# An mLSTM chunk updates its state right behind the numerators, and turns its normalised rows behind the next dense tile

## The chip, the cores and the metric

The kernel runs on one core of a Trainium2 chip. TensorE (PE) multiplies matrices; VectorE (DVE), ScalarE (ACT) and GpSimd (POOL) work on tiles; SyncE (SP) issues most of the transfers between HBM and the on-chip memory SBUF. PSUM holds the products of TensorE until another engine has read them. The metric is the time of one execution on the device in microseconds, as the median of several runs.

## The reference

The reference is one inference step of a decoder of two layers, for 1,024 prompt tokens and 8 samples of one token each. Layer 0 projects the normalised input once, runs a Mamba-2 scan (16 heads) and an mLSTM scan (4 heads of 256) side by side, and projects both together; layer 1 is an RWKV-7 time mixing; a SwiGLU stands behind each. The change concerns the mLSTM scan over chunks of 128 tokens, of which this is the core (c and n are the carried state):

```python
s = einsum('bthd,bshd->btsh', qc, kc) * exp(dlog - m_t[:, :, None])
num = einsum('btsh,bshv->bthv', s, vc) + w_inter[..., None] * einsum('bthd,bhdv->bthv', qc, c)
den = sum(s, axis=2) + w_inter * einsum('bthd,bhd->bth', qc, n)
h = num / maximum(abs(den), exp(-m_t))[..., None]
...
c = dc[..., None, None] * c + einsum('bshd,bshv->bhdv', ws[..., None] * kc, vc)
n = dc[..., None] * n + einsum('bsh,bshd->bhd', ws, kc)
```

Each head's 256 values of h are then normalised by their root mean square, gated and projected.

## The kernel before

Everything runs on one core, layer after layer. The large products are dense tiles of 128 output rows (`dense_tile`), each in three passes of a high and a low part (`mm3`): 24 matmuls for one block of columns, three blocks of 344 columns (72 matmuls) in the z and o tiles of the input projection, one block of 512 in the out tiles of the output projection. Dense tiles use a ring of three PSUM buffers (psd), everything else in layer 0 a ring of five (psb, through `bank`).

The eight mLSTM chunks are strewn among the dense tiles, in this order: chunk 0, three z tiles, chunk 1, three z tiles, a part of the Mamba output, chunk 2, four o tiles, chunk 3, four o tiles, chunk 4, eight out tiles, chunk 5, `mix_ml` (which reads the rows of chunks 0 to 3), eight out tiles, chunk 6, and, from within the first SwiGLU, chunk 7 and the samples.

A chunk (`ml_chunk`) does the following. It loads its queries, keys and values and two broadcast rows of gate logarithms, BM and WI. DVE computes `ws` from the last column of BM, ACT its exponential; POOL and ACT turn BM into the decay matrix. TensorE computes the scores (`sc`, L689), turns the keys into rows (`kT`), and computes the four numerators (`num`, L709 and, from chunk 1 on, L712 with the state `Cst`); each lies in a bank of its own, with the denominator as its last column. For each head ACT takes the absolute value of the denominator into `dn`, DVE copies the numerator into `hr` (L714), and ACT sums its squares into `ss` (with `junk` as the discarded output). `ml_norm_tok` then computes one factor per row and head from `dn` and `ss`: five short operations of DVE (L145, L658) and a logarithm and an exponential on ACT. DVE multiplies `hr` by it, head by head (L151). TensorE turns the rows in eight transposes into two banks (`hT`, L724), ACT copies them to SBUF (L725), and a transfer stores them to HBM. Last, eight products `cu` (L731), two for each head, carry the state forward: each is evacuated by DVE, in chunk 0 as a copy into `Cst` (L734), later by one operation that scales the old state and adds the product (L148).

The buffers: qc, BM and WI have two each, so the load for chunk c+2 begins when chunk c has read its own for the last time; hr, hT, kc, va, vw and the transposed keys have one each. The order of instructions on each engine isn't the order of the program text: a scheduler replays the program against a model of the engines and lists each engine's instructions by when they could start there, with the text's order as priority. Every engine then starts its instructions in the listed order, and each waits for what it needs. Names in the trace carry no chunk numbers: `hr`, `cu` and so on stand for all chunks. L145, L148 and L151 are helpers (`tt`, `stt`, `ts`) that issue one operation each, and L154 is `act`; L186 is the matmul in `mm3`.

Of the kernel before, what the change touches and what calls it, by code (L numbers as in the profile page):

```python
# [8 lines left out]
F32 = mybir.dt.float32  # L9
# [15 lines left out]
LCH = 128  # L25
# [65 lines left out]
def _body(tc, nc, I, O, top):  # L91
# [20 lines left out]
    V, S, G, PE, SY = nc.vector, nc.scalar, nc.gpsimd, nc.tensor, nc.sync  # L112
    dma = SY.dma_start
# [20 lines left out]
    ident = cst("ident")  # L134
# [3 lines left out]
    def bank(name):  # L138
        return P_.b.tile([128, 512], F32, name=name, tag="bank")
# [7 lines left out]
    def stt(out, a, s, b, op0=ALU.mult, op1=ALU.mult, e=None):  # L147
        (e or V).scalar_tensor_tensor(out=out, in0=a, scalar=s, in1=b, op0=op0, op1=op1)  # L148

    def ts(out, a, s1, op0=ALU.mult, s2=None, op1=ALU.bypass, e=None):  # L150
        (e or V).tensor_scalar(out=out, in0=a, scalar1=s1, scalar2=s2, op0=op0, op1=op1)  # L151
# [14 lines left out]
    def wload(src, name, n=1024, step=128, e=None, th=TA_, p=128):  # L166
# [11 lines left out]
                out.append((hi[0:p, q:q + step], lo[0:p, q:q + step]))  # L178
        return out

    def mm3(ps, terms):
        n = 3 * len(terms)
        i = 0
        for w, x in terms:
            for a, b in ((0, 1), (1, 0), (0, 0)):
                PE.matmul(out=ps, lhsT=w[a], rhs=x[b], start=i == 0, stop=i == n - 1)  # L186
                i += 1

    def dense_tile(w, xs, name, evac, m=128, blocks=NBLK, base=0, th=TA_):

        for n0, n in blocks:
            ps = th.bank(f"ps_{name}_{n0}")
            o = ps[0:m, 0:n]
            c = slice(n0 - base, n0 - base + n)
            mm3(o, [(wk, (x[0][:, c], x[1][:, c])) for wk, x in zip(w, xs)])
            evac(n0, n, o)

    def dbank(name):
        return psd.tile([128, 512], F32, name=name, tag="d")
# [455 lines left out]
    def ml_norm_tok(dn, ss, enm, rows, name):  # L655

        tt(dn, dn, enm, ALU.max)
        V.reciprocal(out=dn, in_=dn)  # L658
        tt(ss, ss, dn)
        tt(ss, ss, dn)  # L660
        act(ss, ss, AF.Ln, scale=1.0 / 256, bias=eps[0:rows, :])
        act(ss, ss, AF.Exp, scale=-0.5)
        tt(ss, ss, dn)

    def ml_chunk(c):
# [40 lines left out]
        for h in range(4):  # L706
# [6 lines left out]
            act(dn[:, h:h + 1], b[:, 256:257], AF.Abs)  # L713
            V.tensor_copy(out=hr[:, h, :], in_=b[:, 0:256])  # L714
            act(junk, hr[:, h, :], AF.Square, accum_out=ss[:, h:h + 1])
        ml_norm_tok(dn, ss, tokb[:, c, 32:36], 128, f"{c}")
        for h in range(4):
            ts(hr[:, h, :], hr[:, h, :], ss[:, h:h + 1])
        hT = mp_.tile([128, 8, 128], F32, name=f"hT{c}", tag="hT", bufs=1)
        for hf in range(2):  # L720
            b = bank("hT")
            for q in range(4):
                i = hf * 4 + q
                PE.transpose(b[:, q * 128:q * 128 + 128], hr[:, i // 2, (i % 2) * 128:(i % 2) * 128 + 128], ident)  # L724
            S.copy(hT[:, hf * 4:hf * 4 + 4].rearrange("p c d -> p (c d)"), b)  # L725
        dma(out=HMT[:, :, t0:t0 + LCH], in_=hT)
        for h in range(4):
            for k in range(2):
                b = bank("cu")
                o = b[:, 0:257]  # L730
                PE.matmul(out=o, lhsT=ktok[:, (2 * h + k) * 128:(2 * h + k) * 128 + 128], rhs=vw[:, h, :],  # L731
                          start=True, stop=True)
                if c == 0:
                    V.tensor_copy(out=Cst[:, h, k, :], in_=o)  # L734
                else:
                    stt(Cst[:, h, k, :], Cst[:, h, k, :], WI[:, h, 127:128], o, ALU.mult, ALU.add)


    def ml_decode(dp):
# [21 lines left out]
        qms = [mp_.tile([128, 8, 32], F32, name=f"qm{i}", tag=f"qm{i}", bufs=1) for i in range(2)]  # L761
        for qm in qms:
            G.memset(qm, 0.0)
        hsr = mp_.tile([128, 256], F32, name="hsr", tag="hr", bufs=1)
        nc_acc = mp_.tile([128, 257], F32, name="nc_acc", tag="nc_acc", bufs=1)
        yield
        for b_ in range(8):
# [1046 lines left out]
```

## Time and profile before

| | us |
|---|---|
| median of 3 runs | 3504.39 (3503.94 to 3506.5) |
| profiled execution, its own time | 3510.93 |
| span of the profiled execution | 3509.2 |
| TensorE busy in the span | 3245.9 |
| VectorE busy | 2333.7 |
| ScalarE busy | 1653.4 |
| GpSimd busy | 1241.3 |
| from 490 to 870 us, where the mLSTM chunks lie: TensorE waiting for `hr` | 13.2 |

The profile is one execution of the program, and this one took 6.5 us more than the median. Its mean granted TensorE clock was 0.967 of full speed. Rows of a timeline give an instruction's start, its duration and its engine, line, operation and operands; xN at the end is a run of N of them, and the bracket gives the idle time before and what ended it. Rows of windows give, for each stretch, its length and each engine's busy time in it, and at the end the granted clock, the busy share of the DMA engines and their GB/s. Rows of waits give who waited for what, for how long in total, how often, and the longest.

### The profile page before, as it was taken

What the parts mean: (1) busy time and instruction counts of PE and PEld (TensorE: products, weight loads), DVE (VectorE), ACT (ScalarE), POOL (GpSimd) and SP (SyncE); (2) the same over time, 40 slices, a digit from 0 to 9 for tenths busy, and PEclk for the clock granted to TensorE, in tenths of its full rate; (3) what the DMA queues carried; (4) which work ended last, traced back from release to release, by engine and by line L of the source; (5) the groups of instructions that cost most, each with busy time, mean ns of one, the idle gap of its engine ahead of it and who ended that gap; (6) DMA issues with size and microseconds to landing.
All of it is one profiled execution on the core that took longest, in us unless ns stands there. A gap on an engine that the chain in (4) does not pass through costs nothing.

```text
span 3509.2 us, 61245 instructions
## 1 busy us (share of the span) xinstructions
PE 3245.9 (92%) x22615; PEld 3000.7 (86%) x22615; DVE 2333.7 (67%) x4315; ACT 1653.4 (47%) x3701; POOL 1241.3 (35%) x1586
## 2 busy tenths in 40 slices
PE   6998899998999999989999968988989999999998
PEld 6987789877778887779999968987888889999998
DVE  8865744466765477676776686667777776575555
ACT  5444435434243245654454555665555644453223
POOL 3257520121200002254644566237677783000000
PEclk9999999999999999999999989998999999999999
DMA  3467665663663343553333324462433333333232
GB/s 117 123 183 217 212 194 150 185 196 128 224 198 109 96 144 108 183 153 98 102 102 94 99 77 131 133 204 73 116 100 98 100 95 109 125 97 97 85 102 67
DMA packets 399135, 458.26 MB, mean 131 GB/s; under 512 B 154756, under 2 KB 295524, under 8 KB 398708
## 3 DMA queue, kind: packets, MB, share of 16 engines
q1 hardware_dynamic: 398836, 454.34, 43.6%
q8 instruction: 179, 2.93, 0.3%
q14 instruction: 120, 0.98, 0.1%
HBM read 352.10 MB, written 102.07 MB: 129 GB/s over the span
## 4 chain that ended last, share of the span: by engine, by line
PE 48%; DVE 11%; POOL 10%; DMA 7%; ACT 5%; issue 4%; SPq 1%; DVEq 0%; ACTq 0%; POOLq 0%
PE ps_g L186 10%; PE ps_u L186 9%; PE ps_d L186 8%; PE ps_rw L186 6%; POOL X L145 4%; POOL t L145 4%; PE ps_out L186 3%; PE ps_o L186 2%; ACT L154 2%; PE ps_wo L186 1%; PE M L1361 1%; DMA phm<-scr_hmt 1%; PE cu L731 1%; PE sc L1361 1%; DMA obd<-scr_tblk 1%
## 5 line engine op out<-in xcount | busy, mean ns | idle before, releaser
L186 PE MATMUL ps_d<-al,dhi 128*128 128x260 f32 (+2 forms) x1248 | 386.5, 310 | 20.4 <-DVE xa L145 6.3
L186 PE MATMUL ps_d<-ah,dhi 128*128 128x260 f32 (+2 forms) x1248 | 373.9, 300 | 0.0
L186 PE MATMUL ps_d<-ah,dlo 128*128 128x260 f32 (+2 forms) x1248 | 373.6, 299 | 0.0
L145 POOL TENSOR_TENSOR X<-X,t 32x30 f32<-32x30 f32 (+14 forms) x480 | 308.6, 643 | 32.7
L145 POOL TENSOR_TENSOR t<-X 32x30 f32<-32x30 f32 (+14 forms) x480 | 297.6, 620 | 30.5
L186 PEld LDWEIGHTS ps_d<-al,dhi 128*128 128x128 f32 x1248 | 237.9, 191 | 40.5 <-DVE xa L145 10.7
L186 PEld LDWEIGHTS ps_d<-ah,dlo 128*128 128x128 f32 x1248 | 238.3, 191 | 7.3
L186 PEld LDWEIGHTS ps_d<-ah,dhi 128*128 128x128 f32 x1248 | 237.9, 191 | 7.3 <-issue 0.2
L145 DVE TENSOR_TENSOR wlo_g<-raw_g,whi_g 128x512 fp32r<-128x512 f32 (+1 forms) x192 | 143.2, 749 | 112.9 <-ACT whi_g L175 105.7
L948 ACT CAST dhi<-rawd 128x1024 fp32r<-128x1024 f32 x88 | 88.4, 1046 | 211.5 <-PE ps_d L186 204.9
L175 ACT CAST whi_g<-raw_g 128x512 fp32r<-128x512 f32 (+1 forms) x192 | 114.0, 599 | 147.7 <-DMA raw_g<-in_wgu 90.6
L154 ACT ACT_TABLE_LOAD x136 | 174.5, 1283 | 6.4 <-DVE ss L145 4.1
L145 DVE TENSOR_TENSOR wlo_u<-raw_u,whi_u 128x512 fp32r<-128x512 f32 x176 | 134.6, 766 | 58.1 <-ACT whi_u L175 57.2
L175 ACT CAST whi_u<-raw_u 128x512 fp32r<-128x512 f32 x176 | 108.0, 619 | 122.7 <-PE ps_u L186 97.4
L186 PE MATMUL ps_in<-xnl,whi_in 128*128 128x344 f32 x480 | 156.4, 326 | 1.0 <-ACT ext L287 1.0
L186 PE MATMUL ps_in<-xnh,whi_in 128*128 128x344 f32 x480 | 155.7, 324 | 0.0
L186 PE MATMUL ps_in<-xnh,wlo_in 128*128 128x344 f32 x480 | 155.3, 324 | 0.0
L145 DVE TENSOR_TENSOR dlo<-rawd,dhi 128x512 fp32r<-128x512 f32 x176 | 128.2, 782 | 15.6 <-ACT dhi L948 15.6
L145 POOL TENSOR_TENSOR xx<-xa 128x512 f32<-128x512 f32 x8 | 9.7, 1244 | 350.7 <-PE ps_out L186 350.7
L157 ACT CAST ah<-sg 128x260 fp32r<-128x260 f32 (+2 forms) x155 | 67.5, 436 | 139.4 <-DVE sg L148 137.6
L145 POOL TENSOR_TENSOR Bb<-Bc,consts 128x256 f32<-128x256 f32 x64 | 53.7, 839 | 219.5 <-PE M L1361 147.0
L145 DVE TENSOR_TENSOR wlo_rw<-raw_rw,whi_rw 128x512 fp32r<-128x512 f32 x96 | 74.2, 778 | 78.2 <-ACT whi_rw L175 77.3
(959 smaller groups left out, 11950.0 us busy)
## 6 DMA issues: line engine op xcount, KB each, us to landing
raw_g<-in_wgu SPq DMA_DIRECT2D x88, 512.0 KB
raw_u<-in_wgu SPq DMA_DIRECT2D x88, 512.0 KB
rawd<-in_wdn SPq DMA_DIRECT2D x88, 512.0 KB
raw_rw<-in_wrw SPq DMA_DIRECT2D x48, 512.0 KB
raw_o<-in_wout SPq DMA_DIRECT2D x32, 512.0 KB
raw_in<-in_win SPq DMA_DIRECT2D x20, 512.0 KB
D<-scr_acr SPq DMA_DIRECT2D x16, 512.0 KB
Cs<-in_mc SPq DMA_DIRECT2D x16, 512.0 KB
```

Of the source, the lines that this page charges most:

```text
L145: (e or V).tensor_tensor(out=out, in0=a, in1=b, op=op)
L154: S.activation(out, a, f, **kw)
L157: S.copy(hi, src)
L175: S.copy(hi[0:p, 0:m], raw[0:p, c0:c0 + m])
L186: PE.matmul(out=ps, lhsT=w[a], rhs=x[b], start=i == 0, stop=i == n - 1)
L731: PE.matmul(out=o, lhsT=ktok[:, (2 * h + k) * 128:(2 * h + k) * 128 + 128], rhs=vw[:, h, :], start=True, stop=True)
L948: S.copy(hi, raw)
L1361: PE.matmul(out=b[:, o + q * 128:o + q * 128 + 128], lhsT=lhs(q), rhs=rhs(q), start=True, stop=True)
```

## The change

The eight `cu` products and their evacuation stand directly behind the numerators in the text, ahead of the norm. The chunk ends with the scaling of `hr`, and puts the chunk's number and `hr` into a list, `ml_rest`. What followed (the transposes, the two copies and the store) is a function of its own, `ml_out`, which is called at the end of the next `dense_tile`; each transpose is told to be listed behind that tile's last matmul (`tc.issue_after`). A buffer of the samples' part, `hsr`, which shared the place of `hr`, has one of its own. Each engine issues as many instructions as before.

```diff
--- before.py
+++ after.py
@@ -178,12 +178,15 @@
                 out.append((hi[0:p, q:q + step], lo[0:p, q:q + step]))
         return out
 
+    newest = Ctx()
+    ml_rest = []
+
     def mm3(ps, terms):
         n = 3 * len(terms)
         i = 0
         for w, x in terms:
             for a, b in ((0, 1), (1, 0), (0, 0)):
-                PE.matmul(out=ps, lhsT=w[a], rhs=x[b], start=i == 0, stop=i == n - 1)
+                newest.mm = PE.matmul(out=ps, lhsT=w[a], rhs=x[b], start=i == 0, stop=i == n - 1)
                 i += 1
 
     def dense_tile(w, xs, name, evac, m=128, blocks=NBLK, base=0, th=TA_):
@@ -194,6 +197,8 @@
             c = slice(n0 - base, n0 - base + n)
             mm3(o, [(wk, (x[0][:, c], x[1][:, c])) for wk, x in zip(w, xs)])
             evac(n0, n, o)
+        while ml_rest:
+            ml_out()
 
     def dbank(name):
         return psd.tile([128, 512], F32, name=name, tag="d")
@@ -713,17 +718,6 @@
             act(dn[:, h:h + 1], b[:, 256:257], AF.Abs)
             V.tensor_copy(out=hr[:, h, :], in_=b[:, 0:256])
             act(junk, hr[:, h, :], AF.Square, accum_out=ss[:, h:h + 1])
-        ml_norm_tok(dn, ss, tokb[:, c, 32:36], 128, f"{c}")
-        for h in range(4):
-            ts(hr[:, h, :], hr[:, h, :], ss[:, h:h + 1])
-        hT = mp_.tile([128, 8, 128], F32, name=f"hT{c}", tag="hT", bufs=1)
-        for hf in range(2):
-            b = bank("hT")
-            for q in range(4):
-                i = hf * 4 + q
-                PE.transpose(b[:, q * 128:q * 128 + 128], hr[:, i // 2, (i % 2) * 128:(i % 2) * 128 + 128], ident)
-            S.copy(hT[:, hf * 4:hf * 4 + 4].rearrange("p c d -> p (c d)"), b)
-        dma(out=HMT[:, :, t0:t0 + LCH], in_=hT)
         for h in range(4):
             for k in range(2):
                 b = bank("cu")
@@ -734,6 +728,24 @@
                     V.tensor_copy(out=Cst[:, h, k, :], in_=o)
                 else:
                     stt(Cst[:, h, k, :], Cst[:, h, k, :], WI[:, h, 127:128], o, ALU.mult, ALU.add)
+        ml_norm_tok(dn, ss, tokb[:, c, 32:36], 128, f"{c}")
+        for h in range(4):
+            ts(hr[:, h, :], hr[:, h, :], ss[:, h:h + 1])
+        ml_rest.append((c, hr))
+
+    def ml_out():
+
+        c, hr = ml_rest.pop()
+        t0 = c * LCH
+        hT = mp_.tile([128, 8, 128], F32, name=f"hT{c}", tag="hT", bufs=1)
+        for hf in range(2):
+            b = bank("hT")
+            for q in range(4):
+                i = hf * 4 + q
+                with tc.issue_after(newest.mm.ins):
+                    PE.transpose(b[:, q * 128:q * 128 + 128], hr[:, i // 2, (i % 2) * 128:(i % 2) * 128 + 128], ident)
+            S.copy(hT[:, hf * 4:hf * 4 + 4].rearrange("p c d -> p (c d)"), b)
+        dma(out=HMT[:, :, t0:t0 + LCH], in_=hT)
 
 
     def ml_decode(dp):
@@ -761,7 +773,7 @@
         qms = [mp_.tile([128, 8, 32], F32, name=f"qm{i}", tag=f"qm{i}", bufs=1) for i in range(2)]
         for qm in qms:
             G.memset(qm, 0.0)
-        hsr = mp_.tile([128, 256], F32, name="hsr", tag="hr", bufs=1)
+        hsr = mp_.tile([128, 256], F32, name="hsr", tag="hsr", bufs=1)
         nc_acc = mp_.tile([128, 257], F32, name="nc_acc", tag="nc_acc", bufs=1)
         yield
         for b_ in range(8):
```

What this does to the listed order is seen on VectorE in chunk 0. In these rows L145 with `ss0` is the last step of the norm, L151 the scaling of chunk 0's rows, `ws2` belongs to chunk 2 and needs its load of BM, and L734 is the evacuation of `cu`. Before:

```order
L145 TENSOR_TENSOR wlo_z7512_5206<-raw_z7_5199,whi_z7512_5205 128x512
L145 TENSOR_TENSOR ss0_4519<-ss0_4519,dn0_4518 128x4
L151 TENSOR_SCALAR hr0_4517<-hr0_4517,ss0_4519 128x256 x4
L145 TENSOR_TENSOR ws2_5429<-tokb_107,BM2_5425 128x4
L148 SCALAR_TENSOR_TENSOR zth_5137<-zth_5137,ps_z6_0_5112 128x344
L734 COPY Cst_4451<-cu_4566 128x257
L734 COPY Cst_4451<-cu_4569 128x257
L734 COPY Cst_4451<-cu_4572 128x257
```

And with the change, where that evacuation is L728:

```order
L728 COPY Cst_4451<-cu_4544 128x257
L145 TENSOR_TENSOR wlo_z7512_5206<-raw_z7_5199,whi_z7512_5205 128x512
L728 COPY Cst_4451<-cu_4547 128x257
L145 TENSOR_TENSOR ss0_4519<-ss0_4519,dn0_4518 128x4
L728 COPY Cst_4451<-cu_4550 128x257
L145 TENSOR_TENSOR ws2_5429<-tokb_107,BM2_5425 128x4
L151 TENSOR_SCALAR hr0_4517<-hr0_4517,ss0_4519 128x256
L728 COPY Cst_4451<-cu_4553 128x257
L151 TENSOR_SCALAR hr0_4517<-hr0_4517,ss0_4519 128x256 x3
L728 COPY Cst_4451<-cu_4556 128x257
```

Four evacuations now stand ahead of the scaling, and `ws2`, which stood behind it, stands ahead of it.

TensorE around the same place. Before, the transposes (L724) come first, then the first of the products, in the second block of z tile 6:

```order
L186 MATMUL ps_z6_344_5141<-xnh3_125,wlo_z60_5105 128x344
L186 MATMUL ps_z6_344_5141<-xnh3_125,whi_z60_5104 128x344
L724 MATMUL hT_4553<-consts_75,hr0_4517 128x128 x4
L724 MATMUL hT_4559<-consts_75,hr0_4517 128x128 x4
L731 MATMUL cu_4566<-vw0_4515,ktok0_4501 128x257
L731 MATMUL cu_4569<-vw0_4515,ktok0_4501 128x257
L731 MATMUL cu_4572<-vw0_4515,ktok0_4501 128x257
L186 MATMUL ps_z6_344_5141<-xnl4_128,whi_z6512_5108 128x344
L186 MATMUL ps_z6_344_5141<-xnh4_127,wlo_z6512_5109 128x344
L186 MATMUL ps_z6_344_5141<-xnh4_127,whi_z6512_5108 128x344
```

With the change (transposes L746, products L725, matmuls of dense tiles L189) the products end ahead of the transposes, and these stand near the end of the first block of that tile, earlier in the stream of dense matmuls:

```order
L189 MATMUL ps_z6_0_5112<-xnh5_129,wlo_z6512_5109 128x344
L725 MATMUL cu_4559<-vw0_4515,ktok0_4501 128x257
L189 MATMUL ps_z6_0_5112<-xnh5_129,whi_z6512_5108 128x344
L189 MATMUL ps_z6_0_5112<-xnl6_132,whi_z6512_5108 128x344
L189 MATMUL ps_z6_0_5112<-xnh6_131,wlo_z6512_5109 128x344
L725 MATMUL cu_4562<-vw0_4515,ktok0_4501 128x257
L189 MATMUL ps_z6_0_5112<-xnh6_131,whi_z6512_5108 128x344
L189 MATMUL ps_z6_0_5112<-xnl7_134,whi_z6512_5108 128x344
L746 MATMUL hT_4674<-consts_75,hr0_4517 128x128 x2
L189 MATMUL ps_z6_0_5112<-xnh7_133,wlo_z6512_5109 128x344
L189 MATMUL ps_z6_0_5112<-xnh7_133,whi_z6512_5108 128x344
L746 MATMUL hT_4674<-consts_75,hr0_4517 128x128 x2
L746 MATMUL hT_4680<-consts_75,hr0_4517 128x128 x4
```

The third place is VectorE in chunk 5, where `ws7` needs the load of chunk 7's BM. Before:

```order
L145 TENSOR_TENSOR ss5_6902<-ss5_6902,dn5_6901 128x4 x2
L145 TENSOR_TENSOR wlo_o012512_7168<-raw_o012_7161,whi_o012512_7167 128x512
L145 TENSOR_TENSOR ws7_7787<-tokb_107,BM7_7783 128x4
L145 TENSOR_TENSOR ss5_6902<-ss5_6902,dn5_6901 128x4
L151 TENSOR_SCALAR hr5_6900<-hr5_6900,ss5_6902 128x256 x4
L145 TENSOR_TENSOR wlo_o0130_7200<-raw_o013_7197,whi_o0130_7199 128x512
L145 TENSOR_TENSOR xa_1_6430<-xa_1_6430,ps_out011_0_7135 128x512
L145 TENSOR_TENSOR wlo_o013512_7204<-raw_o013_7197,whi_o013512_7203 128x512
```

And with the change:

```order
L145 TENSOR_TENSOR wlo_o012512_7168<-raw_o012_7161,whi_o012512_7167 128x512
L148 SCALAR_TENSOR_TENSOR Cst_4451<-Cst_4451,WI5_6866,cu_6935 128x257
L145 TENSOR_TENSOR ws7_7787<-tokb_107,BM7_7783 128x4
L145 TENSOR_TENSOR ss5_6902<-ss5_6902,dn5_6901 128x4
L151 TENSOR_SCALAR hr5_6900<-hr5_6900,ss5_6902 128x256 x3
L148 SCALAR_TENSOR_TENSOR Cst_4451<-Cst_4451,WI5_6866,cu_6938 128x257
L151 TENSOR_SCALAR hr5_6900<-hr5_6900,ss5_6902 128x256
L148 SCALAR_TENSOR_TENSOR Cst_4451<-Cst_4451,WI5_6866,cu_6941 128x257
L148 SCALAR_TENSOR_TENSOR Cst_4451<-Cst_4451,WI5_6866,cu_6944 128x257
L148 SCALAR_TENSOR_TENSOR Cst_4451<-Cst_4451,WI5_6866,cu_6947 128x257
```

`ws7` stands ahead of the scaling in both; behind it there are now, between the scalings, the evacuations of the third `cu` product and the ones that follow.

Orders change in layer 1 too, whose text is the same. On GpSimd, where `X07` is an inversion step by step and `xc1l3` the low part of an input of a product (L145), the rows before are:

```order
L145 TENSOR_TENSOR xc1l1_21097<-lp121512_21427,xc1h1_21096 128x260
L145 TENSOR_TENSOR xc1l3_21101<-lp123512_21435,xc1h3_21100 128x260
L1315 MEMSET X07_22318 32x32
L145 TENSOR_TENSOR t307_22321<-X07_22318 32x30
L145 TENSOR_TENSOR X07_22318<-X07_22318,t307_22321 32x30
L145 TENSOR_TENSOR t307_22321<-X07_22318 32x58
L145 TENSOR_TENSOR X07_22318<-X07_22318,t307_22321 32x29x2
L1121 COPY whi_g2100_21553<-wlo_g2100_21554 32x128
```

And with the change:

```order
L145 TENSOR_TENSOR xc1l1_21097<-lp121512_21427,xc1h1_21096 128x260
L1327 MEMSET X07_22318 32x32
L145 TENSOR_TENSOR t307_22321<-X07_22318 32x30
L145 TENSOR_TENSOR X07_22318<-X07_22318,t307_22321 32x30
L145 TENSOR_TENSOR t307_22321<-X07_22318 32x58
L145 TENSOR_TENSOR X07_22318<-X07_22318,t307_22321 32x29x2
L145 TENSOR_TENSOR t307_22321<-X07_22318 32x84
L145 TENSOR_TENSOR X07_22318<-X07_22318,t307_22321 32x28x3
L145 TENSOR_TENSOR t307_22321<-X07_22318 32x108
L145 TENSOR_TENSOR X07_22318<-X07_22318,t307_22321 32x27x4
L145 TENSOR_TENSOR xc1l3_21101<-lp123512_21435,xc1h3_21100 128x260
```

`xc1l3` goes from ahead of the inversion's first steps to behind the eighth of them.

## The prediction

> **What bounds the kernel now.** I read the page first, then what TensorE waits for while the chunks run.
>
> ```profile
> PE 3245.9 (92%) x22615; PEld 3000.7 (86%) x22615; DVE 2333.7 (67%) x4315; ACT 1653.4 (47%) x3701; POOL 1241.3 (35%) x1586
> ...
> PE hT L724 <- DVE hr L151: 13.2, 8, 3.1
> PE ps_g L186 <- DVE f00l L145: 4.9, 4, 2.8
> PE n_ps L212 <- DVE n_acc L145: 1.9, 1, 1.9
> ```
>
> TensorE is busy for 92% of the span, so only its idle time and its clock can be won. The three rows of waits are from 490 to 870 us, where all eight chunks lie: the transposes wait 13.2 us for the scaled rows, longer than for anything else there. That is 0.38% of the run, and the most that this wait alone can give.
>
> The timeline of TensorE puts these waits in chunks 0, 1, 2, 3, 5 and 6 (in brackets the idle time before the row; chunks 4 and 7 have none):
>
> ```profile
> 512.64 1.16 PE L724 MATMUL hT<-consts,hr 128*128 128x128 f32 x8 [1.47 <-DVE hr L151]
> ...
> 542.54 1.72 PE L724 MATMUL hT<-consts,hr 128*128 128x128 f32 x8 [2.41 <-DVE hr L151]
> 544.05 2.54 PE L731 MATMUL cu<-vw,ktok 128*128 128x257 f32 x6
> ...
> 617.37 0.44 PE L724 MATMUL hT<-consts,hr 128*128 128x128 f32 x2 [0.42 <-DVE hr L151]
> 618.64 0.44 PE L724 MATMUL hT<-consts,hr 128*128 128x128 f32 x2 [0.84 <-DVE hr L151]
> 619.85 0.63 PE L724 MATMUL hT<-consts,hr 128*128 128x128 f32 x4 [0.77 <-DVE hr L151]
> ...
> 649.08 1.16 PE L724 MATMUL hT<-consts,hr 128*128 128x128 f32 x8 [1.89 <-DVE hr L151]
> 650.07 1.47 PE L731 MATMUL cu<-vw,ktok 128*128 128x257 f32 x6
> ...
> 754.52 1.94 PE L724 MATMUL hT<-consts,hr 128*128 128x128 f32 x8 [3.07 <-DVE hr L151]
> 756.25 2.25 PE L731 MATMUL cu<-vw,ktok 128*128 128x257 f32 x6
> ```
>
> The stalls of 2.41 and 3.07 us cost more than themselves: eight transposes behind them take 1.72 and 1.94 us where they take 1.16 behind 1.89 us of waiting, and six update matmuls 2.54 and 2.25 for 1.47. Each time that is 1.6 us (0.56 + 1.07, and 0.78 + 0.78). The granted clock (PEclk, the last column but two) says why:
>
> ```profile
> 512.00:520.00 8.00, 7.26 (x41) 6.40 (x42) 4.00 (x13) 2.49 (x6) 2.33 (x2) 1.00 0.50 159
> 540.00:548.00 8.00, 5.59 (x26) 4.96 (x26) 3.42 (x10) 4.44 (x8) 0.00 (x0) 0.79 0.34 107
> 647.00:655.00 8.00, 6.11 (x37) 5.51 (x36) 4.68 (x12) 4.28 (x8) 0.00 (x0) 1.00 0.51 143
> 751.00:759.00 8.00, 4.93 (x19) 4.04 (x19) 6.59 (x13) 4.29 (x9) 2.30 (x2) 0.79 0.81 276
> 803.00:813.00 10.00, 4.36 (x17) 2.98 (x15) 5.44 (x18) 9.39 (x23) 0.00 (x0) 0.63 0.00 1
> ```
>
> So in these chunks a stall of 1.89 us leaves the clock at 1.00, one of 2.41 brings it to 0.79. I put the step at 2.2 us, their middle.
>
> **What holds the scaled rows back** is on VectorE, whose instructions start in the order in which they are listed:
>
> ```profile
> 514.74 0.17 DVE L145 TENSOR_TENSOR ws<-tokb,BM 128x4 f32<-128x4 f32 x1 [1.45 <-DMA BM<-scr_bmr]
> ...
> 542.04 1.14 DVE L151 TENSOR_SCALAR hr<-hr,ss 128x256 f32<-128x256 f32 x4
> ...
> 616.88 0.17 DVE L145 TENSOR_TENSOR ws<-tokb,BM 128x4 f32<-128x4 f32 x1 [1.23 <-DMA BM<-scr_bmr]
> 616.96 3.00 DVE L151 TENSOR_SCALAR hr<-hr,ss 128x256 f32<-128x256 f32 x4
> ...
> 751.60 0.17 DVE L145 TENSOR_TENSOR ws<-tokb,BM 128x4 f32<-128x4 f32 x1 [2.46 <-DMA BM<-scr_bmr]
> 752.21 0.92 DVE L145 TENSOR_TENSOR ss<-ss,dn 128x4 f32<-128x4 f32 x1 [0.44 <-ACT ss L154]
> 753.16 2.00 DVE L151 TENSOR_SCALAR hr<-hr,ss 128x256 f32<-128x256 f32 x4
> ```
>
> The scaling waits for the chain of the norm (ss), and, where `ws` of chunk c+2 stands ahead of it in that order, for the load of that chunk's BM too. BM has two buffers, and the load into one can start only when the numerators that read it are done. Its landing therefore follows the numerators, whatever stands behind them on TensorE.
>
> **The change part by part.** Nothing is added or removed: each engine issues as many instructions as before. Moved are eight update products per chunk (from behind the transposes to behind the numerators, each with its VectorE update), eight transposes, the two ScalarE copies and the store behind them. The store's first reader is mix_ml behind chunk 5, and only of chunks 0 to 3; I cost its move at nothing (and a stall like the rows above if it came late). The own buffer for hsr costs memory only.
>
> The gain is cover: updates need nothing from the norm. Their loss is cover too: the scheduler now puts the transposes behind fewer dense matmuls. By the two orders the dense matmuls between numerators and transposes go from 50 to 36 (chunk 0), 45 to 33, 40 to 30, 51 to 28, 62 to 53, 37 to 30 (chunk 5). The prices:
>
> ```profile
> 504.12 0.32 PE L186 MATMUL ps_z<-xnh,wlo_z 128*128 128x344 f32 x1
> 508.49 0.32 PE L186 MATMUL ps_z<-xnh,whi_z 128*128 128x344 f32 x1
> 749.67 0.39 PE L186 MATMUL ps_out<-mixbh,wlo_o 128*128 128x512 f32 x1
> 751.05 0.40 PE L186 MATMUL ps_out<-mixbh,wlo_o 128*128 128x512 f32 x1
> L731 PE MATMUL cu<-vw,ktok x128: 377/380/635, 513.6 to 856.8; 128*128 128x257 f32 x128
> L148 DVE SCALAR_TENSOR_TENSOR Cst<-Cst,WI,cu x56: 470/481/484, 545.2 to 857.7; 128x257 f32<-128x257 f32 x56
> ```
>
> The first two lie 28 starts apart, 0.156 us for a z or o matmul; the next two six, 0.23 for an out matmul. An update product is two passes (x128 for 64 products); six passes in 1.47 with a last one of 0.38 give 0.218 a pass, 0.435 a product, 3.5 for eight.
>
> Chunk 1: TensorE fell idle at 542.54 − 2.41 = 540.13. Without 12 matmuls (1.9) and with 3.5 of updates it is 541.7, so the stall is 0.8, below the step: 2.41 + 1.6 become 0.8. **+3.2.**
>
> Chunk 0: idle came at 511.17; without 14 (2.2) and with 3.5 it is 512.5. But ws2, which stood behind the scaling, now stands ahead of it, so the scaling waits for BM2: 514.74 + 0.17, and the transposes start 0.5 behind it as in chunk 1 (542.04 to 542.54), at 515.4. Stall 2.9 for 1.47, and a lowered clock, 1.6, that was not there. **−3.1.** Bounds: +1.5 if BM2 has landed by then, −3.1.
>
> Chunks 2 and 3: in chunk 2 the last product needs a bank, and the update that frees it (the third) is listed behind ws4 and three scalings: 616.88 + 0.17 + 2.25 + 0.48 = 619.8, where TensorE is through at 618.4: 1.4, and some 0.5 more for the rest, against 2.03. In chunk 3, 23 fewer (3.6) for 3.5: 2.0 against 1.89. Together **+0.1**, no clock; if both passed the step, −3.2.
>
> Chunk 5: idle at 751.45; 7 fewer (1.6), seven products more (3.0), 752.9. The eighth waits for the third update, behind ws7, ss and three scalings: 753.16 + 1.50 + 0.48 = 755.1, so 2.2, and 0.5 more for the fourth update behind the last scaling. 2.7 in two parts, with half the clock term, 3.5, for 3.07 + 1.6. **+1.2**, between 0.4 and all of it, 4.7.
>
> Chunk 6 runs with the norm of the feed-forward and has little dense work beside it:
>
> ```profile
> 806.53 0.58 PE L186 MATMUL ps_g<-f00l,whi_g 128*128 128x256 f32 x1 [0.85 <-DVE f00l L145]
> 810.35 0.58 PE L186 MATMUL ps_g<-f00l,whi_g 128*128 128x256 f32 x1 [2.81 <-DVE f00l L145]
> 814.56 0.66 PE L724 MATMUL hT<-consts,hr 128*128 128x128 f32 x2 [2.34 <-DVE hr L151]
> ...
> 809.58 0.16 DVE L145 TENSOR_TENSOR ss<-ss,dn 128x4 f32<-128x4 f32 x1 [2.58 <-ACT junk L154]
> ```
>
> TensorE idles 0.85, 2.81 and 2.34 us here, and VectorE itself 2.58 in the middle one. The eight products, 3.5 us that ran behind the transposes, fit into these pauses, and five of their updates (2.4) into VectorE's. **+3.5**; 0 if the updates hold up f00l, on which TensorE waits 2.81, and 5 at the lowered clock, where a product costs more.
>
> Chunks 4 and 7: no stall now; by the counts chunk 4 goes from 62 × 0.23 = 14.3 us of cover to 12.2 + 3.5: nothing.
>
> Sum: 3.2 − 3.1 + 0.1 + 1.2 + 3.5 = 4.9 us. The profiled execution took 3510.93, 6.5 above the median; 3506.0 by it, **3499.5** on the median's scale. Its own range, with about half of the bounds met together: 3492 to 3506.
>
> The clock terms rest on 0.79 behind 2.41 us. The Trainium skill, "TensorE: Matmul & The Clock Gate" (Part 1, The HAM clock gate), lets the clock fall only after about 3.4 us of idle. By that no stall here would lower it, and the sum would be −1.5 + 1.6 + 0.1 + 0.4 + 3.5 = 4.1; the two windows at 0.79 disagree, and I go by them.
>
> **The rivals.**
>
> B, all the waits go: the updates cover the norm in every chunk and BM arrives in time. 13.2 us and two clock terms, 3.2: 16.4, **3488.0**. For it: eight products are 3.5 us, and no stall is longer than 3.07. Against: the dense cover shrinks by 1.6 to 3.6 us in the same chunks.
>
> C, slower: the updates queue on VectorE behind the wait for BM. They hold the banks, of which products, scores and transposes share five, so in chunks 0, 1, 2, 3 and 5 TensorE stands until BM is there, at chunk 0's and 5's size of 2.7 us, and each stall passes the step. 5 × (2.7 + 1.6) = 21.5, where now 10.9 (1.47 + 2.41 + 2.03 + 1.89 + 3.07) and 3.2 are lost: 7.4 more, **3511.8**, if chunk 6 brings nothing. It decides once the stalls are over 2.2. For it: the orders of chunks 2 and 5 have updates behind ws. Against: in chunk 1 ws3 stands so early that the scaling of 542.04 does not wait for it.
>
> D, the rest of the program moves: the orders also differ in layer 1, which the edit does not touch. There TensorE has more idle time than in all chunks:
>
> ```profile
> 2000.00:2600.00 600.00, 508.71 (x3941) 484.67 (x3940) 435.37 (x824) 347.34 (x858) 339.17 (x480) 0.92 0.41 118
> ...
> PE ps_rw L186 <- POOL xc1l L145: 1.8, 2, 1.3
> ```
>
> 91.3 us idle; the second row is one place (2100 to 2130) where TensorE waits for GpSimd's xc1l, and xc1l3 now stands behind eight steps of an inversion that it stood ahead of. A tenth of the 91.3 either way, 9.1, gives **3508.6** or 3490.4. Nothing says which.
>
> **How the numbers follow.** A measurement of this kernel tells 0.2%, 7.0 us, from no change: faster is below 3497.4, slower above 3511.4. The forecast has 0.45 (0.16 faster, 0.27 same, 0.02 slower), B 0.22 (all faster), C 0.17 (0.11 slower, 0.06 same, as 3511.8 is at the border), D 0.16 (0.05, 0.04, 0.07, since disorder costs more easily). Faster 0.43, same 0.37, slower 0.20. The range 3484 to 3513 takes in B and C with a few us about them; of D only the far ends are left out.
>
> **What would show it.** Right: hT waits 0.8 us in chunk 1 and near 3 in chunk 0, with `ws<-BM` directly ahead of the scaling; a clock of 1.00 near chunk 1 and below it near chunk 0; update products between the ps_g rows of chunk 6; 2000 to 3500 as long as before. Wrong: waits of TensorE for Cst above 3 us (C), no wait for hr anywhere (B), or a difference that lies behind 2000 us (D).

## The result: 0.6% slower, in two places

| | before | changed |
|---|---|---|
| median, first comparison | 3506.91 us | 3528.11 us |
| ratio, with its 95% interval | | 1.0059 (1.0042 to 1.0076) |
| median, second comparison | 3504.77 us | 3528.46 us |
| ratio, with its 95% interval | | 1.0067 (1.0052 to 1.0083) |
| profiled executions, their own times | 3510.93 us | 3521.58 and 3529.02 us |

The change costs 21 to 24 us; a gain of 5 was forecast, and the time lies outside the range. The page of the changed kernel shows no other work, only a longer span:

```profile
span 3519.8 us, 61240 instructions
...
PE 3249.3 (92%) x22615; PEld 3000.2 (85%) x22615; DVE 2327.3 (66%) x4315; ACT 1653.1 (47%) x3701; POOL 1229.6 (35%) x1586
```

Where the time goes is seen by following the same matmul (say, the 172nd of ps_g) in two profiles and subtracting its starts. The table gives this lag behind the profile of before, in us, at places of the program (time in before's profile); it is worked out from the timelines of TensorE.

| at | 480, ahead of chunk 0 | 558, behind 1 | 668, behind 3 | 786, behind 5 | 936, behind 7 | 1237 | 1980 | 2370 | 3060 | 3457 |
|---|---|---|---|---|---|---|---|---|---|---|
| changed | +1.2 | +5.6 | +7.4 | +5.9 | +8.1 | +7.0 | -1.9 | -3.9 | +13.1 | +11.1 |
| changed, second profile | -0.2 | +4.0 | +5.9 | +6.2 | +8.0 | +6.9 | 0.0 | -3.9 | +20.7 | +18.5 |

Three stretches move. The chunks lose 7 to 8 us. Between 1237 and 1980 the lag falls by 7 to 9, but it falls by 5 to 12 in every kernel below that is set against this profile, so this is time that the profiled execution of before lost there itself (it was 6.5 over its median). And from 2370 to 3060, in layer 1, whose text the change doesn't touch, 17 to 25 us are lost.

First the chunks. The waits of TensorE in the changed kernel, 490 to 870 us:

```profile
PE hT L746 <- DVE hr L151: 9.0, 5, 3.4
PE ps_g L189 <- DVE f00l L145: 6.2, 5, 2.8
PE cu L725 <- DVE Cst L148: 4.7, 3, 2.2
```

The wait of the transposes fell from 13.2 to 9.0, and 4.7 us of a new one came: the state's products wait for a bank that an evacuation frees. Together 13.7, hardly more than before, so the sizes of these two waits alone don't make the 7 to 8 us. Chunk 0 has grown worst; its transposes on TensorE, and what VectorE did:

```profile
516.76 0.69 PE L746 MATMUL hT<-consts,hr 128*128 128x128 f32 x2 [3.40 <-DVE hr L151]
518.04 0.69 PE L746 MATMUL hT<-consts,hr 128*128 128x128 f32 x2
519.16 0.69 PE L746 MATMUL hT<-consts,hr 128*128 128x128 f32 x2 [0.42 <-DVE hr L151]
521.06 0.69 PE L746 MATMUL hT<-consts,hr 128*128 128x128 f32 x2 [1.22 <-DVE hr L151]
...
516.27 0.17 DVE L145 TENSOR_TENSOR ws<-tokb,BM 128x4 f32<-128x4 f32 x1 [2.21 <-DMA BM<-scr_bmr]
516.36 0.34 DVE L151 TENSOR_SCALAR hr<-hr,ss 128x256 f32<-128x256 f32 x1
516.62 0.42 DVE L728 COPY Cst<-cu 128x257 f32<-128x257 f32 x1
516.96 4.05 DVE L151 TENSOR_SCALAR hr<-hr,ss 128x256 f32<-128x256 f32 x3
```

VectorE stands at ws for 2.21 us until BM lands, as forecast. What was not forecast is the row behind it: three scalings take 4.05 us, where the first takes 0.34 and four took 1.14 in chunk 0 before. The landing of BM has set GpSimd to work at the same moment, and the granted clock of TensorE falls to 0.50 (windows from 512 to 530 us, clock in the last column but two):

```profile
516.52 1.31 POOL L145 TENSOR_TENSOR BM<-BM,consts 128x512 f32<-128x512 f32 x1 [12.27 <-DVE ws L145]
517.91 1.04 POOL L145 TENSOR_TENSOR BM<-BM,tokb 128x512 f32<-128x512 f32 x1
518.91 1.95 POOL L145 TENSOR_TENSOR vw<-va,ws 128x1028 f32<-128x1028 f32 x1
...
512.00:517.00 5.00, 1.60 (x9) 1.26 (x8) 1.22 (x6) 1.71 (x4) 0.48 (x1) 0.86 0.62 223
517.00:522.00 5.00, 3.33 (x13) 2.04 (x13) 5.00 (x8) 1.66 (x4) 3.78 (x3) 0.50 0.02 7
522.00:530.00 8.00, 8.00 (x46) 7.92 (x46) 1.11 (x3) 1.45 (x3) 2.38 (x1) 0.76 0.53 153
```

Then layer 1. One wait of the changed kernel from 2450 to 3060 us stands in both its profiles with the same 9.4 us and hardly at all in the kernels that keep the old order there (0.4 with the state update alone, the first of the experiments below that changes the kernel). How much of the loss it is worth is taken up at the end of the part on the prediction:

```profile
PE ysd L1553 <- DVE sg L148: 9.4, 3, 4.5
```

### The profile page after: what moved, and what is told of

It reads as the page before. It is cut to its first block, busy times and chain, and to the rows that moved or that the text cites. A ratio compares the mean times of both kernels' runs of the same rounds, so it can differ in the third digit from the quotient of the medians.

```text
span 3519.8 us, 61240 instructions
## 1 busy us (share of the span) xinstructions
PE 3249.3 (92%) x22615; PEld 3000.2 (85%) x22615; DVE 2327.3 (66%) x4315; ACT 1653.1 (47%) x3701; POOL 1229.6 (35%) x1586
## 4 chain that ended last, share of the span: by engine, by line
PE 56%; DVE 14%; DMA 9%; POOL 8%; ACT 7%; issue 4%; SPq 2%; DVEq 0%; ACTq 0%; POOLq 0%
PE ps_g L189 10%; PE ps_d L189 10%; PE ps_u L189 9%; PE ps_rw L189 6%; PE ps_in L189 3%; POOL t L145 3%; POOL X L145 3%; PE ps_out L189 3%; PE ps_o L189 2%; ACT L154 2%; PE ps_z L189 2%; PE ps_wo L189 1%; PE M L1373 1%; DMA phm<-scr_hmt 1%; DVE lp L148 1%
## 5 line engine op out<-in xcount | busy, mean ns | idle before, releaser
L189 PE MATMUL ps_d<-al,dhi 128*128 128x260 f32 (+2 forms) x1248 | 387.3, 310 | 21.0 <-DVE xc L145 7.5
L189 PE MATMUL ps_d<-ah,dlo 128*128 128x260 f32 (+2 forms) x1248 | 374.8, 300 | 0.0
L189 PE MATMUL ps_d<-ah,dhi 128*128 128x260 f32 (+2 forms) x1248 | 374.7, 300 | 0.0
L145 POOL TENSOR_TENSOR X<-X,t 32x30 f32<-32x30 f32 (+14 forms) x480 | 303.3, 632 | 32.2
L145 POOL TENSOR_TENSOR t<-X 32x30 f32<-32x30 f32 (+14 forms) x480 | 289.9, 604 | 31.0
L189 PEld LDWEIGHTS ps_d<-al,dhi 128*128 128x128 f32 x1248 | 239.1, 192 | 40.7 <-DVE xc L145 11.3
L189 PEld LDWEIGHTS ps_d<-ah,dlo 128*128 128x128 f32 x1248 | 239.4, 192 | 7.4
L189 PEld LDWEIGHTS ps_d<-ah,dhi 128*128 128x128 f32 x1248 | 239.0, 192 | 7.6 <-issue 0.6
L145 DVE TENSOR_TENSOR wlo_g<-raw_g,whi_g 128x512 fp32r<-128x512 f32 (+1 forms) x192 | 145.2, 759 | 108.8 <-ACT whi_g L175 107.1
L145 DVE TENSOR_TENSOR wlo_u<-raw_u,whi_u 128x512 fp32r<-128x512 f32 x176 | 136.9, 779 | 60.9 <-ACT whi_u L175 59.7
L189 PE MATMUL ps_in<-xnl,whi_in 128*128 128x344 f32 x480 | 156.6, 327 | 0.8 <-ACT ext L292 0.8
L189 PE MATMUL ps_in<-xnh,whi_in 128*128 128x344 f32 x480 | 156.0, 325 | 0.0
L189 PE MATMUL ps_in<-xnh,wlo_in 128*128 128x344 f32 x480 | 155.4, 324 | 0.0
L145 DVE TENSOR_TENSOR dlo<-rawd,dhi 128x512 fp32r<-128x512 f32 x176 | 125.5, 767 | 16.6 <-ACT dhi L960 16.6
L145 POOL TENSOR_TENSOR Bb<-Bc,consts 128x256 f32<-128x256 f32 x64 | 52.1, 814 | 232.6 <-PE M L1373 158.6
L145 POOL TENSOR_TENSOR xx<-xa 128x512 f32<-128x512 f32 x8 | 9.7, 1243 | 347.5 <-PE ps_out L189 347.5
L145 DVE TENSOR_TENSOR wlo_rw<-raw_rw,whi_rw 128x512 fp32r<-128x512 f32 x96 | 72.2, 758 | 81.6 <-ACT whi_rw L175 80.7
```

Of the source, the lines that this page charges most:

```text
L145: (e or V).tensor_tensor(out=out, in0=a, in1=b, op=op)
L189: newest.mm = PE.matmul(out=ps, lhsT=w[a], rhs=x[b], start=i == 0, stop=i == n - 1)
```

## The experiments

Theory 1 held that the chunks lose it all, theory 2 that the order that layer 1 got does. The listed orders themselves tell what can be taken apart. Putting off the transposes of chunks 0 to 5 and 7, on top of the state update, changes nothing in any list. Putting off chunk 6 alone, on top of the state update, gives the changed kernel's lists exactly. So the change has two parts: the state update, which orders chunks 0 to 5, and chunk 6's transposes, with which the order of layer 1 moves. They aren't independent: each alone gives layer 1 an order that the changed kernel doesn't have.

**The changed kernel again**, without an edit.

> The changed kernel once more, for a second profile and more times. Both theories expect a ratio to before of 1.004 to 1.008. Of the difference in the profile (10.6 us) the chunks showed 6.4 (from +1.2 us ahead of chunk 0 to +7.6 us behind chunk 7) and the stretch from 1250 us on showed -11.8 and then +19. Theory 1 (the loss is in the chunks) expects the lag behind chunk 7 to be 5 to 8 us again, and the lag gathered behind it to differ by 10 us or more from the first profile, since it would be chance. Theory 2 (the order of layer 1 costs) expects 8 us or more of lag gathered behind 1250 us again.

1.0067 (1.0052 to 1.0083); lag of 8.0 us behind chunk 7, and 24.6 from 2370 to 3060, after 17.0 the first time. Both places are real; that the loss in layer 1 is chance, as theory 1 had it, is not borne out, though its size differs by 7.6 us between two profiles of one kernel.

**The state update alone**

```diff
         for h in range(4):
             ts(hr[:, h, :], hr[:, h, :], ss[:, h:h + 1])
         ml_rest.append((c, hr))
+        ml_out()
...
-                with tc.issue_after(newest.mm.ins):
+                if True:
                     PE.transpose(...)
```

> The state update ahead of the norm and the transposes, and the transposes directly behind the scaling, not behind the next dense tile. The listed order is that of the changed kernel in chunks 0 to 5 word for word; in layer 1 it is that of before except for 79 rows of TensorE between rows 10912 and 11143. Theory 1 (chunks): as slow as the changed kernel, 1.004 or more, with a lag of 4 to 8 us behind chunk 5. Theory 2 (layer 1): 4 to 7 us over before (1.001 to 1.002), and nothing more gathered behind 900 us.

1.0015 (1.0004 to 1.0027): 5 us, and the changed kernel, on the same chip, 17 more (3511.04 and 3528.46). The lag behind chunk 7 is 9.5 us, as in the changed kernel, and from 2370 to 3060 it goes from +0.9 to -0.3. Theory 2 is right on where most is lost; the chunks have their 5.

**Chunk 6's transposes alone**: the kernel before, and only chunk 6 puts its transposes off (the program text around them as in the changed kernel, the state update last as before).

```diff
-        ml_rest.append((c, hr))
+        ml_rest.append((c, hr))
+        if c not in (6,):
+            ml_out()
...
-                with tc.issue_after(newest.mm.ins):
+                with (tc.issue_after(newest.mm.ins) if c in (6,) else ExitStack()):
```

> The kernel before with one thing changed: chunk 6 puts its transposes behind the next dense tile. Chunks 0 to 5 keep their order; layer 1 is dealt a third way (3581 of TensorE's rows differ from before). Theory 1 (chunks): within 0.15% of before. Theory 2 (layer 1): 0.2% or more away from before on either side, with the difference gathered behind 2000 us.

1.0003 (0.9993 to 1.0012). Layer 1 has a third order here (3581 of TensorE's rows stand elsewhere than before), and it costs nothing over the whole: theory 2's number for this run is a miss, and theory 1's, within 0.15% of before, is met. The lag goes from -7.6 to +2.2 between 2370 and 3060, and ends at -0.6 at 3457, where the state update alone ends at -0.5. A new order need not be a worse one. Chunk 6's transposes stand in rows 3865 to 3872 of TensorE's list, exactly where the changed kernel has them, so putting them off does not by itself cost the 17 us.

**All transposes behind the second dense tile**: another way of putting them off in the program text, which leaves layer 1's order as with the state update alone but for 80 of TensorE's rows.

```diff
-        while ml_rest:
+        newest.k = getattr(newest, 'k', 0) + 1 if ml_rest else 0
+        while ml_rest and newest.k > 1:
             ml_out()
+            newest.k = 0
...
-                with tc.issue_after(newest.mm.ins):
+                if True:
```

> The changed kernel with the transposes of every chunk called at the end of the second dense tile behind it, and without the rule that lists them behind that tile's last matmul. TensorE's list then differs from that of the state update alone in 202 rows (chunks 6 and 7 and 80 rows of layer 1). Theory 1 (putting the transposes off is what costs): as the changed kernel, 1.005 or more of before. Theory 2 (the order that layer 1 got is what costs): as the state update alone, 1.000 to 1.003, with no more than 3 us gathered behind 1000 us against it.

1.0020 (1.0010 to 1.0030), with a lag from 2370 to 3060 that goes from -2.9 to -0.7: theory 2's number. For chunk 6 this run tests nothing, though: the scheduler lists its transposes in rows 3806 to 3826 of TensorE, as with the state update alone, and only those of chunks 3 and 7 later. With the run before it, the reading is this: the old order of layer 1 goes with no loss there, chunk 6's transposes put off go with none over the whole, and the order that the changed kernel got goes with the 17 us.

**A third buffer for BM**, with the state update alone:

```diff
-        BM = mp_.tile([128, 4, 128], F32, name=f"BM{c}", tag="BM")
+        BM = mp_.tile([128, 4, 128], F32, name=f"BM{c}", tag="BM", bufs=3)
```

> As the state update alone, and three buffers for BM in place of two, so that the load for chunk c+2 need not wait for the numerators of chunk c. If the wait of ws for BM, now ahead of the scaling, is what costs in chunks 0, 2 and 5, the idle time of 3.40 us in chunk 0 goes to under 1.5 and the two waits for Cst (2.12 and 2.21) to under 1, and the run is 4 to 8 us shorter than with the state update alone. If the norm on ScalarE is the limit, less than 2 us.

0.9958 (0.9943 to 0.9973), 20 us under the state update alone, where 4 to 8 were expected. The waits from 490 to 870 us, first with two buffers, then with three:

```profile
PE hT L747 <- DVE hr L151: 11.7, 9, 3.0
PE cu L725 <- DVE Cst L148: 6.0, 3, 3.5
```

```profile
PE hT L747 <- DVE hr L151: 2.4, 3, 1.5
PE hT L747 <- DVE Cst L728: 2.1, 1, 2.1
...
PE cu L725 <- DVE Cst L148: 1.4, 1, 1.4
```

17.7 us of waits became 5.9, and at 936 us the lag is 14.8 us less (+9.5 and -5.3). The two profiled executions are 15.5 us apart (3510.43 and 3494.95), so nearly all of that lies in the chunks; the 20 are of the medians, and the same kernel run again below is 16 under by the ratios. Not all that was expected came: chunk 0's longest wait went from 2.96 to 2.1 us, not under 1.5, and now it is for the evacuations of `cu`; of the two long waits for Cst one is gone and one is 1.4.

The buffer does more than let the load start earlier: the scheduler deals the chunks' lists anew with it. 231 rows of TensorE and 169 of VectorE stand elsewhere, and in chunk 0 `ws` starts at 508.09 without a wait, with 16 operations of VectorE between it and the scaling at 516.97. This run can't tell the earlier load from the new order; the run with ws on GpSimd, below, leaves the lists nearly alone.

**The same buffer in the kernel before**, run twice:

```diff
-        BM = mp_.tile([128, 4, 128], F32, name=f"BM{c}", tag="BM")
+        BM = mp_.tile([128, 4, 128], F32, name=f"BM{c}", tag="BM", bufs=3)
```

> The kernel before with three buffers for BM and nothing else; layer 1 keeps its order. With the state update moved, the third buffer took 20 us (3511.0 to 3491.1). Theory A (the wait for BM holds the scaling in both kernels): the stalls of chunks 0 to 5 shrink here too, and the run is 8 to 14 us shorter than before (0.996 to 0.998). Theory B (BM free, the cover by the state update is what gains): 1 to 5 us shorter at most, with waits for hr of 8 us or more left in the chunks.

0.9968 (0.9954 to 0.9981), 12 us under before. The transposes' wait for hr falls from 13.2 to this, with the state update last as before (571 of TensorE's rows in the chunks are listed elsewhere here):

```profile
PE hT L724 <- DVE hr L151: 4.5, 2, 2.3
```

> The kernel before with three buffers for BM, on the same chip as the next: 0.996 to 0.998 again. Its lag behind chunk 7 was 11.2 us under before, that of the state update with three buffers 5.3 us under it, so by the profiles it should be the shorter by up to 6 us; by the medians so far (0.9968 and 0.9958) the longer by 3.

> The state update with three buffers for BM, next to the run before it: 0.995 to 0.998. If moving the state update is worth anything once the wait for BM is gone, it is 0.1% or more under the run before it.

On one chip: 0.9973 (0.9962 to 0.9984) in the old place and 0.9970 (0.9957 to 0.9982) in the new one, 3494.02 and 3494.30 us. With BM free, the place of the state update makes no difference that these runs can tell; the 0.1% that was asked of it is not there. Both beat both kernels; the smaller edit is the buffer alone.

**The third buffer in the changed kernel** (the same edit):

> The changed kernel with three buffers for BM; its layer 1 has the order of the changed kernel. If the chunks and layer 1 add up, it is the state update with three buffers (3491.1) plus the 17 us by which the changed kernel is over the state update alone: 3506 to 3511, 1.000 to 1.002 of before. If the loss in layer 1 came from a lag of the chunks, it would be at 3488 to 3494.

1.0004 (0.9992 to 1.0017), 3506.79, in the range of 3506 to 3511 that follows if the parts add up, the chunks and the order of layer 1. The wait of ysd for sg stands at 9.4 us here too, though the chunks have no lag left (-5.8 at 936), so it belongs to the order, not to what comes from the chunks.

**ws on GpSimd**, with the state update alone and two buffers. The lists stay as they were but for ws itself and, in chunk 4, 8 rows of TensorE, 17 of VectorE and 10 of ScalarE.

```diff
-        tt(ws, lib, BM[:, :, 127], ALU.add)
+        tt(ws, lib, BM[:, :, 127], ALU.add, G)
```

> The state update alone, where GpSimd computes ws and not VectorE; two buffers for BM as before. All other lists stay as they were but for 8 rows of TensorE; GpSimd waits for the same BM anyway, to add the mask. Theory A (VectorE stands at ws until BM lands, and the scaling and the state's evacuations behind it): 8 to 20 us shorter than the state update alone (0.996 to 0.9995 of before), and waits for Cst and hr in chunks 0 to 5 under 4 us in all, where they were 17.7. Theory B (the late BM itself, through the decay matrix, is what costs): within 3 us of the state update alone.

0.9987 (0.9978 to 0.9996), 3500.33, some 10 us under the state update alone. GpSimd now stands at ws until BM lands, at 515.62 in chunk 0, and VectorE doesn't. Its scaling starts at 513.31, right behind the norm, and is done ahead of GpSimd's work on BM:

```profile
512.89 0.16 DVE L145 TENSOR_TENSOR ss<-ss,dn 128x4 f32<-128x4 f32 x1 [1.86 <-ACT ss L154]
...
513.31 0.34 DVE L151 TENSOR_SCALAR hr<-hr,ss 128x256 f32<-128x256 f32 x1
513.57 0.42 DVE L728 COPY Cst<-cu 128x257 f32<-128x257 f32 x1
513.90 0.87 DVE L151 TENSOR_SCALAR hr<-hr,ss 128x256 f32<-128x256 f32 x3
...
515.62 0.21 POOL L145 TENSOR_TENSOR ws<-tokb,BM 128x4 f32<-128x4 f32 x1 [12.05 <-DMA BM<-scr_bmr]
515.90 1.27 POOL L145 TENSOR_TENSOR BM<-BM,consts 128x512 f32<-128x512 f32 x1
```

That is theory A by its time: what stands at the head of VectorE's list is a cost, with BM as late as before. By its waits it is half a miss: 10.1 us for hr and Cst where under 4 were expected, so the place of ws is not all that holds them. The lag behind chunk 7 is -1.5 for +9.5. In chunk 0 two things went together, the wait at ws and the scalings beside GpSimd; the run doesn't say how much is whose.

**Another bank for ysd**, in the changed kernel and, as a control, with the state update alone:

```diff
-        b = psd.tile([128, 512], F32, name=f"ysd{i}", tag="d")
+        b = pbank(f"ysd{i}")
```

> The changed kernel, where the 16 products ysd of the samples in layer 1 take a bank of the other ring, not of the three of the dense tiles. Layer 1 keeps its order up to row 13639 of TensorE and is dealt anew from there. If the waits of ysd for sg (9.4 us in three) are what costs in layer 1, the run is 9 to 14 us shorter than the changed kernel, 1.002 to 1.004 of before. If the loss is spread over the whole new order, less than 5 us shorter or longer.

> The control of the run before it: the same edit of ysd in the kernel with the state update alone, which does not show the wait for sg. If only that wait matters, within 0.1% of the state update alone (1.0005 to 1.0025 of before); if each new order of layer 1 is a draw of its own, up to 10 us either way.

1.0114 (1.0098 to 1.0130) and 1.0083 (1.0069 to 1.0097): both far slower, some 18 and 25 us over the kernels they start from. Both expectations are misses. The wait for sg is gone (waits of 2.6 to 3.1 us for d_y have come), but the ring that was to take the products belongs to the scan, and layer 1 was dealt anew from row 13639 of TensorE on. The edit can't show what the 9.4 us are worth.

## Why the prediction was wrong, step by step

Two steps failed. The larger one: the sum has no term for layer 1. The prediction saw that its order changes, wrote that nothing says which way, left it to rival D and put it at nothing; the runs put 17 us there. The other: the chunks were to gain 4.9 us and lost 7 to 8, in chunk 0 because the scaling was priced as it runs without GpSimd beside it, in chunk 6 because work moved into TensorE's pauses was counted as time won. One by one:

**That only TensorE's idle time and clock can be won** held: the work is the same in every kernel here, and every gain and loss is in TensorE's waits or in how long the same work takes it.

**Chunk 1** was forecast at a stall of 0.8 us for 2.41 with no clock term, and **chunk 0** at 2.9 for 1.47 with one. Chunk 1 measured less gain, chunk 0 more loss:

```profile
544.82 1.23 PE L746 MATMUL hT<-consts,hr 128*128 128x128 f32 x8 [1.51 <-DVE hr L151]
```

1.51 us, and eight transposes in 1.23, so the clock is whole. In chunk 0 the mechanism was right, ws2 ahead of the scaling and its wait for BM, and the size was not: 3.40 + 0.42 + 1.22 = 5.0 us. The step that failed is "the transposes start 0.5 behind it as in chunk 1": that price came from scalings without GpSimd beside them, and here the load that frees VectorE frees GpSimd too. The slow scaling was among the prediction's own rows (616.96, 3.00 us for four); it priced chunk 2 with it and chunk 0 without. The clock term of 1.6 was too small as well, for a clock of 0.50 over 5 us and 0.76 over the next 8. Together the two chunks lost 4.2 to 4.4 us where +0.1 was forecast.

**Chunks 2 and 3** were put at +0.1 and lost 1.8 to 1.9:

```profile
625.61 0.70 PE L725 MATMUL cu<-vw,ktok 128*128 128x257 f32 x2 [2.12 <-DVE Cst L148]
...
649.37 0.70 PE L746 MATMUL hT<-consts,hr 128*128 128x128 f32 x4 [2.45 <-DVE hr L151]
```

Chunk 2's products wait where the prediction put them, on the third evacuation behind ws4 and three scalings, 2.1 us for 1.4 + 0.5. Chunk 3 was put at 2.0; it measured 2.45, and 0.37 more for Cst.

**Chunk 5** was right in its first part: 2.2 us for the wait of the last product was forecast, and 2.21 measured. The second part, 0.5 us, did not come; the transposes behind it start without a wait.

```profile
763.14 0.70 PE L725 MATMUL cu<-vw,ktok 128*128 128x257 f32 x2 [2.21 <-DVE Cst L148]
```

With chunk 4 it gained 1.5 us in the first profile and lost 0.3 in the second, where 1.2 was forecast; two profiles of one kernel that lie 1.8 apart can't confirm such a term.

**Chunk 6** was the largest term, +3.5, on the reading that products fill TensorE's pauses. They did run there, from 809 on, and the transposes' wait of 2.34 is gone; but the waits for f00l grew, from 4.9 us to 6.2:

```profile
808.44 0.70 PE L217 MATMUL n_ps<-n_acc,consts 128*128 128x256 f32 x2 [1.49 <-DVE n_acc L145]
814.73 0.39 PE L189 MATMUL ps_g<-f00l,whi_g 128*128 128x256 f32 x1 [0.38 <-DVE f00l L145]
818.11 0.39 PE L189 MATMUL ps_g<-f00l,whi_g 128*128 128x256 f32 x1 [2.76 <-DVE f00l L145]
819.70 0.58 PE L189 MATMUL ps_g<-f00l,whi_g 128*128 128x256 f32 x1 [0.96 <-DVE f00l L145]
822.56 0.58 PE L189 MATMUL ps_g<-f00l,whi_g 128*128 128x256 f32 x1 [1.85 <-DVE f00l L145]
```

From 786 to 1237 us of before's time, with chunk 7 in it, TensorE idles 3.9 us less than before (16.1 and 12.2, over the same 2173 matmuls) and is busy 5.1 longer; right behind these waits, from 826 to 836, its granted clock is 0.82, where it was 1.00 at that place before. So the pauses were filled in part, and the time was not won. That the chain of the norm through ScalarE and VectorE sets the end of this stretch is how these rows read; no run tests it. Chunks 6 and 7 lost 1.8 to 2.2 us in the changed kernel and gained 0.3 with the state update alone, where the products run in the same pauses. The bound of 0 for this term was the value to take.

**Rival C** (updates queue behind the wait for BM, all stalls grow) named the mechanism that ws on GpSimd then showed (VectorE stands at ws, and what is behind it waits too), with 7.4 us; with the state update alone 5.3 us were measured by the ratio, 6.3 by the medians. It had all five stalls grow and pass the step of the clock, which they didn't. It had a chance of 0.17, against a forecast that rested on the same rows. The argument against it, that ws3 in chunk 1 stands early, holds for chunks 3 and 4 as well (ws at 641.85, the scaling at 648.97); in chunks 0, 2 and 5 ws stands directly ahead of the scaling or one operation from it.

**Rival D** (layer 1 is dealt anew) had 0.16, 9.1 us and no sign. It is the larger part: 17 us by the medians of the changed kernel and the state update alone. Its size was taken as a tenth of TensorE's idle time in the 600 us to 2600, while the loss lies mostly behind 2370, up to 3060, and includes stalls that weren't there before and so were in no idle time. The place that the prediction picked, xc1l3 on GpSimd, was not it: at 2370 us the lag has fallen, not grown. Range and chances took C and D one at a time; both came, on the same side, and the range ended at 3513.

**What stays open** is how layer 1 loses its time. This much is shown. Up to 3200 us, where the lists have come together again, it loses 14.6 and 22.0 us in the two profiles. The same stretch before and in these two (length, TensorE's busy time, and the clock in the last column but two):

```profile
2370.00:3200.00 830.00, 768.84 (x6299) 740.06 (x6298) 594.53 (x1200) 426.57 (x998) 420.42 (x620) 0.96 0.36 102
2366.10:3210.70 844.60, 773.11 (x6295) 744.96 (x6294) 590.80 (x1201) 425.40 (x999) 410.67 (x619) 0.96 0.35 100
2366.10:3218.10 852.00, 781.12 (x6296) 752.46 (x6295) 591.79 (x1200) 425.85 (x999) 408.82 (x618) 0.94 0.34 99
```

TensorE idles 61.2, 71.5 and 70.9 us: 10 more in both. The other 4 and 12 it is busy longer with the same matmuls, at a lower clock in the second profile. With the changed order ysd waits three times for sg, 9.4 us in each of three profiles. The longest, in rows of TensorE and VectorE of the changed kernel:

```profile
2670.62 1.46 PE L1553 MATMUL ysd<-d_r,dSt 64*64 64x1 f32 x16 [4.52 <-DVE sg L148]
...
2663.67 2.30 DVE L145 TENSOR_TENSOR y<-y,gr 128x512 f32<-128x512 f32 x1 [1.43 <-POOL y L145]
...
2668.62 1.63 DVE L1266 TENSOR_TENSOR_SCAN cs<-rmask,thw 128x512 f32<-128x512 f32 x1
2670.18 0.39 DVE L148 SCALAR_TENSOR_TENSOR sg<-sg,ps_u 128x256 f32<-128x256 f32 x1
```

The products need a bank that the evacuation into sg frees, and VectorE's list has six other operations ahead of it. Behind this wait the clock is lower too: 0.50 over the 6 us from 2670, and the sixteen products take 1.46 us where they take 0.88 with the state update alone. But 9.4 is not the net loss, for the old order has waits that the changed one lacks. From 2450 to 3060 us, before and changed:

```profile
PE M L1361 <- DVE Z L1396: 8.4, 9, 3.1
...
PE M L1373 <- DVE Z L1408: 0.3, 1, 0.3
```

And with chunk 6's transposes alone ysd waits 3.4 us for sg, without a loss over the whole. So which waits of the new order make the 10 us is not shown; the one edit that took the wait of ysd away dealt the rest of the layer anew and was slower.

## What to carry to other kernels

Before moving work into the shadow of a wait, look at what stands at the head of the waiting engine's own list: here one operation of 0.17 us, waiting for a load that was due two chunks later, held the rows that mattered. A third buffer for that load, with the order that the scheduler then dealt, was worth 9 to 12 us without any change to the program's order of work. Where a scheduler lists the whole program, an edit in one place deals other places anew; compare the lists first, and test the edit in a form that leaves them alone, because that part can be larger than the edit. Work moved into an engine's pause is not time won by itself: from chunk 6 on TensorE idled less and was no earlier.

## What the runs showed of the hardware beyond what was expected

VectorE's scaling of 128 x 256 values takes 0.34 us by itself, and three take 4.05 while GpSimd runs its operations on BM and vw; in the run with ws on GpSimd three take 0.87, ahead of that work. One by one the three of 4.05 take 1.03, 1.19 and 1.98 us, and each ends 0.14 to 0.16 us behind the end of one of GpSimd's three rows (517.83, 518.95 and 520.86), as if it had waited for that whole operation. The Trainium skill, "GPSIMD Engine Reference" (Specifications), states that GpSimd's interfaces to SBUF are shared with VectorE and that they contend with some kinds of VectorE instruction; these rows agree.

The step of the clock at 2.2 us of idle time did not hold as a threshold: in chunk 3 a stall of 2.45 us left the clock whole, where 2.41 lowered it in chunk 1 of before. The second half of that chunk's transposes and the window behind it:

```profile
650.55 0.66 PE L746 MATMUL hT<-consts,hr 128*128 128x128 f32 x4
...
648.00:656.00 8.00, 6.63 (x44) 6.44 (x45) 3.23 (x10) 2.58 (x7) 0.64 (x1) 1.00 0.32 76
```

The same stall of chunk 3 lowered the clock in two other runs, with the state update alone and with ws on GpSimd:

```profile
650.02 1.11 PE L747 MATMUL hT<-consts,hr 128*128 128x128 f32 x4 [2.44 <-DVE hr L151]
648.00:656.00 8.00, 5.98 (x32) 5.92 (x33) 3.22 (x10) 2.71 (x7) 1.28 (x1) 0.79 0.21 58
...
640.08 0.70 PE L747 MATMUL hT<-consts,hr 128*128 128x128 f32 x4 [2.45 <-DVE hr L151]
638.00:646.00 8.00, 5.92 (x30) 5.73 (x31) 3.23 (x10) 2.63 (x6) 1.35 (x1) 0.79 0.19 54
```

After 3.40 us in chunk 0 it fell to 0.50. So near 2.4 us the same stall can cost a clock or not; the prediction should have carried that as a range in each chunk. The Trainium skill, "TensorE: Matmul & The Clock Gate" (Part 1, The HAM clock gate), calls the window in which idleness is judged free-running, which would make the outcome hang on where a stall falls in it; the stalls of 2.41 to 2.45 agree with that, though they are shorter than the page's window of about 3.4 us.
